# Ordering the second-layer loads behind the loads of h, and splitting up four tile turns, in an encoder layer on one core

## The chip, the core and the metric

The kernel runs on one core of a Trainium2 chip. The metric is the device time of one execution, in microseconds (us); the time before is the median of three runs, 2369.57 us (2364.59 to 2371.45).

## What is computed

One layer of a bidirectional encoder on 1024 tokens of width 1024, all in float32. Two of its four steps matter here, both feed-forward networks with a hidden width of 2816:

```python
def swiglu(x, w1, w3, w2):
    return (jax.nn.silu(x @ w1) * (x @ w3)) @ w2

x = layer_norm(ALPHA * x + 0.5 * swiglu(x, ffn1_w1, ffn1_w3, ffn1_w2), ln1_g, ln1_b)
...   # attention and a state-space branch, merged, then LN2
x = layer_norm(ALPHA * x + 0.5 * swiglu(x, ffn2_w1, ffn2_w3, ffn2_w2), ln3_g, ln3_b)
...   # a gated embedding, then LN4
```

## The kernel before, in words

**Products.** Every float32 matrix is held as a high and a low part (`split`, L62 to L65: the high part by ScalarE, the low part by VectorE), and a product is three TensorE matmuls: high by high, high by low, low by high. A matmul is 128x128 by 128x512. The large products use a seven-product scheme over 2x2 blocks, so each feed-forward matrix is cut in four blocks b11, b12, b21, b22, and sums and differences of blocks are made on VectorE.

**First pass, `ffn_up` (from L278).** For each of 11 column pairs p it forms the hidden values and, in its `finish` (L311), the seven left operands h, which are written to the DRAM tensor `hd` (L320, seven writes for each p). The last writes, of p = 10, are made while the second layer has begun.

**Second pass, `ffn_down` (L345 to L417).** It works through seven stages in the order 1, 5, 6, 3, 7, 2, 4 (`stages`, L377). A stage takes the 11 column pairs in six blocks q (`DUOS`: five of two, one of one). For each block it loads h (L393, `load_raw`, 512 KB, tag `raw`, four buffers), takes a block of w2, in four of the stages makes a difference of w2 blocks in place on VectorE first (L397), splits both, and then issues for each of four banks t the matmuls of L412. The four PSUM banks of a stage are added to `acc` at its end (L367 to L374, line L370). A block of two is 24 matmuls, a stage 132. The w2 blocks are loaded by `fetch` (L355, six loads at L361: four into the tile `w2w`, two into `w2e`): all six loads of b11 ahead of stage 1, of b12 ahead of stage 5, of b22 ahead of stage 6, of b21 ahead of stage 2. They go to tiles of the pools that the first pass frees at its end. The eight `acc` tiles (L549 from x, L975 from x2d) are loaded into the tiles that held the last hidden values; the norm's gain and bias (L110) into one more freed tile. h of block q = 5 in stage 1 can be loaded only when the writes of p = 10 have landed.

**The order of the work.** The program is traced into a scheduler, which fixes the order of each engine's instructions at compile time: an instruction that it takes to be ready goes in front of one that comes earlier in the program and isn't. Here all loads and stores are issued by SyncE (SP), one after the other, in that fixed order, and an instruction that waits holds up all behind it. A block `with tc.issue_after(ins)` keeps the order on one engine: what is traced in it stands behind `ins` in the engine's queue. It adds no wait on a result.

**The beginning of the second feed-forward (`first2`, L924 to L968).** Its input comes out of a layer norm, tile by tile of 128 tokens; `norm_in` (L183) runs the norm of tile j and turns tile j - 4 (`transpose_blocks`, L165: eight 128x128 transposes on TensorE into PSUM, then splits on ScalarE and VectorE into the tiles `xa` for j < 4, and `td` and `tc` for j from 4 on). So four turns, of tiles 4 to 7, are left for `finish` (L197). `first2` makes the first columns by plain products (`plain`, L260: two times 24 matmuls, with a `yield` after each 24): two of half 0, which read only `xa`; then `finish()`, L938, the four turns; then two of half 1, which read `td` and `tc`. Between parts of these it makes differences of `acc` (L176 to L181) and turns those (`turned`, L157).

Of the kernel before, what the change touches and what calls it, by code (L numbers as in the profile page):

```python
# [20 lines left out]
F32 = mybir.dt.float32  # L21
# [24 lines left out]
def layer_kernel(ctx, tc, A):  # L46
# [17 lines left out]
        S.activation(hi, src, AF.Copy)  # L64
        V.tensor_tensor(out=lo, in0=src, in1=hi.bitcast(F32), op=ALU.subtract)  # L65

    def load_raw(src, n=1024):
        raw = wts.tile([128, n], F32, tag="raw", bufs=RAW, name="raw")
        nc.sync.dma_start(raw, src)
        return raw  # L70

    def wload(src, tag="u", pool=None, bufs=None, n=1024):
# [34 lines left out]
    def ln_params(t, g, b):  # L107

        for i, src in enumerate((g, b)):
            nc.sync.dma_start(t[:, i, :], src.to_broadcast([128, D]))  # L110
        return t[:, 0, :], t[:, 1, :]
# [71 lines left out]
    def norm_in(steps, acc, gt, bt, xT, pool, done=None, lag=3, blocks=False):  # L183


        ready = []

        def bring(late):
            j = ready.pop(0)
            if blocks:  # L190
                transpose_blocks(acc, j, xT)
            else:
                transpose_in(acc[j], j, xT, late)
            if done:
                done(j)

        def finish():  # L197
            while ready:
                bring(True)

        for j, sums in steps:
            layer_norm(acc[j], sums, gt, bt, pool)
            ready.append(j)
            if len(ready) > lag:
                bring(False)
        return finish
# [53 lines left out]
    def plain(B, ws, half, row, s):  # L260


        u, g = [pdn.tile([128, 512], F32, tag="dn", name=n) for n in ("pu", "pg")]
        for i, b in enumerate(((B[1], B[2]), (B[4], B[3]))[half]):
            for k in range(4):
                ks = slice(i * 512 + k * 128, i * 512 + k * 128 + 128)
                for o, w in zip((u, g), ws):
                    wh, wl = w[row]
                    for m, (x, y) in enumerate(((wh, 0), (wh, 1), (wl, 0))):
                        PE.matmul(o, lhsT=x[:, ks], rhs=b[y][:, k, :], start=(i == 0 and k == 0 and m == 0),  # L270
                                  stop=(i == 1 and k == 3 and m == 2), skip_group_check=True)
            yield
        S.activation(s, u, AF.Silu)
        V.scalar_tensor_tensor(out=s, in0=s, scalar=0.5, in1=g, op0=ALU.mult, op1=ALU.mult)
# [67 lines left out]
                                   op0=ALU.mult, op1=ALU.mult)  # L342
            finish(p, s1, s2)

    def ffn_down(fp, acc, hd, w2, homes):  # L345

        W, ends = {}, {}
        sums = [sml.tile([128, 2], F32, tag="sums", bufs=8, name="sums") for _ in range(8)]

        def block(i, q):  # L350
            p, n = DUOS[q]
            t, o = (W[i], p) if p < 8 else (ends[i[0]], 3 * i[1] + p - 8)
            return t[:, o:o + n, :]

        def fetch(i):  # L355
            if i[0] not in ends:
                ends[i[0]] = homes["end", i[0]]("w2e", F32)
            W[i] = homes[i]("w2w", F32)
            for q in range(len(DUOS)):
                p, n = DUOS[q]  # L360
                nc.sync.dma_start(block(i, q), w2[i[0], i[1]][:, p:p + n, :])  # L361

        X = [pdn.tile([128, 512], F32, tag="dn", name="pd") for _ in range(4)]
        yt = []
        count = {}

        def add(out, j, n, ps, first, last):  # L367
            a = acc[j][:, n * 512:n * 512 + 512]
            if first or last:
                V.scalar_tensor_tensor(out=a, in0=a, scalar=ALPHA if first else 1.0, in1=ps, op0=ALU.mult, op1=ALU.add,  # L370
                                       accum_out=sums[j][:, n:n + 1] if last else None)
            else:
                V.tensor_tensor(out=a, in0=a, in1=ps, op=ALU.add)

        b11, b12, b21, b22 = (0, 0), (0, 1), (1, 0), (1, 1)

        stages = ((1, 0, True, [(0, 0, True, False)]), (5, 1, True, [(4, 1, True, False)]),  # L377
                  (6, 0, False, [(0, 1, True, False)]), (3, 1, False, [(0, 1, False, True)]),
                  (7, 0, False, [(4, 1, False, True)]), (2, 1, True, [(0, 0, False, True)]),
                  (4, 0, False, [(4, 0, True, True)]))  # L380
        want = {1: b11, 5: b12, 6: b22, 2: b21}
        right = {1: b11, 5: b11, 6: b11, 3: b22, 7: b12, 2: b21, 4: b11}
        less = {5: (b12, b11), 6: (b22, b11), 7: (b22, b12), 4: (b21, b11)}
        for i, bank, fresh, reads in stages:
            if i in want:
                fetch(want[i])
            if bank == 1 and fresh:
                yy = [pup.tile([128, 1024], F32, tag="up", name="pdy") for _ in range(2)]
                Y = [t[:, c:c + 512] for t in yy for c in (0, 512)]
            P = Y if bank else X  # L390
            held = []
            for q, (p, n) in enumerate(DUOS):
                h = load_raw(hd[i - 1][q].rearrange("p a b -> p (a b)")[:, 0:n * 512], n * 512)  # L393
                w = block(right[i], q)
                if i in less:
                    x, y = (block(b, q) for b in less[i])
                    V.tensor_tensor(out=w, in0=x, in1=y, op=ALU.subtract)  # L397
                hh, hl = [wts.tile([128, 1024], F32R, tag=t, name=o) for t, o in (("uh", "hh"), ("ul", "hl"))]
                wh, wl = [fp.tile([128, 1024], F32R, tag="v", bufs=4, name=o) for o in ("wh", "wl")]
                split(h[:, 0:n * 512], hh[:, 0:n * 512], hl[:, 0:n * 512])  # L400
                split(w, *[t[:, 0:n * 512].rearrange("p (a b) -> p a b", a=n) for t in (wh, wl)])
                held.append((p, n, hh, hl, wh, wl))
                if i == 4 and q == 4:
                    continue

                def part(t, first_p=held[0][0]):
                    for p, n, hh, hl, wh, wl in held:
                        for a in range(n):
                            ts = slice(a * 512 + t * 128, a * 512 + t * 128 + 128)
                            ws = slice(a * 512, a * 512 + 512)  # L410
                            for m, (x, y) in enumerate(((hh, wh), (hh, wl), (hl, wh))):
                                PE.matmul(P[t], lhsT=x[:, ts], rhs=y[:, ws], start=(fresh and p + a == 0 and m == 0),  # L412
                                          stop=(p + a == NP - 1 and m == 2), skip_group_check=True)

                for t in range(4):
                    part(t)
                    if q == len(DUOS) - 1:  # L417
                        for j, nn, first, last in reads:
                            add(None, j + t, nn, P[t], first, last)
                        if i == 4:  # L420
                            yield 4 + t, sums[4 + t]
                held = []
                if i == 4 and q < 4:
                    yield q, sums[q]

    def tok(t):
        return t.rearrange("(p j) d -> j p d", j=8)
# [37 lines left out]
    with tc.tile_pool(name="f1", bufs=1, reuse_waits="tile") as fp:  # L465
        def fx(name, dt=F32R, shape=(128, 8, 512)):
            return fp.tile(list(shape), dt, tag="x", bufs=3, name=name)
# [76 lines left out]

        acc = [fp.tile([128, 1024], F32, tag="a", bufs=8, name="acc") for _ in range(8)]
        homes = {(0, 0): fx, ("end", 0): fx, (0, 1): xx, (1, 1): xx, ("end", 1): xx, (1, 0): xx}
        dn = ffn_down(fp, acc, hd, A["ffn1_w2"], homes)
        for j in range(8):
            nc.sync.dma_start(acc[j], tok(A["x"])[j])  # L549

        def spill(j):
            nc.sync.dma_start(x1d[j], acc[j])

        first = next(dn)
        ln = ln_params(fx("ln", F32, (128, 2, 1024)), A["ln1_g"], A["ln1_b"])
        x1T = xtiles()
        finish = norm_in(chain([first], dn), acc, *ln, x1T, fp, spill)
        us = [("w_u", m, AF.Copy, ud) for m in range(4)]
# [365 lines left out]
    def first2():  # L924
# [7 lines left out]
                hl = wload(A[name][row * NP])  # L932
            w[i][row] = hl
        s1, s2 = [wts.tile([128, 1024], F32, tag="raw", bufs=RAW, name="raw") for _ in range(2)]
        for row, s in ((0, s1), (1, s2)):
            for _ in plain(X2b, w, 0, row, s[:, l]):
                pass
        finish()  # L938
        cs = [slice(c * 128, c * 128 + 128) for c in range(4)]
        c, last = 0, []  # L940
        for row, s in ((1, s2), (0, s1)):
# [16 lines left out]
        def ends():  # L958
# [3 lines left out]
            for c in (0, 2):  # L962
                t = turned((acc[c][:, r], acc[c + 1][:, r]))
                for i in range(2):
# [4 lines left out]
    ffn_up(fp, X2b, A["ffn2_w1"], A["ffn2_w3"], hd, first2)  # L969
    acc = [fa.tile([128, 1024], F32, tag="a", bufs=8, name="acc") for _ in range(8)]  # L970

    dn = ffn_down(fp, acc, hd, A["ffn2_w2"], {(0, 0): xx, ("end", 0): xx, (0, 1): xx, (1, 1): xx,
                                               ("end", 1): x16, (1, 0): x16})
    for j in range(8):
        nc.sync.dma_start(acc[j], x2d[j])  # L975
    first = next(dn)
    gt, bt = ln_params(x16("ln", F32, (128, 2, 1024)), A["ln3_g"], A["ln3_b"])
    x3T = [[f(n) for _ in range(2)] for f, n in ((xx, "xhi"), (x16, "xlo"))]
    finish = norm_in(chain([first], dn), acc, gt, bt, x3T, fp, lag=2)
    gt, bt = ln_params(x16("ln", F32, (128, 2, 1024)), A["ln4_g"], A["ln4_b"])  # L980
# [483 lines left out]
```

## Time and profile before

| | |
|---|---|
| median of three runs | 2369.57 us |
| the profiled execution: its time, its span | 2375.43 us, 2373.6 us |
| TensorE matmul busy | 2280.4 us, 96% of the span |
| VectorE busy | 1586.0 us, 67% |
| ScalarE busy | 938.4 us, 40% |
| moved by DMA | 265.63 MB, 112 GB/s over the span |
| mean granted TensorE clock | 0.982 |

The profile is of one execution. Its rows name engines as PE (TensorE matmul), DVE (VectorE), ACT (ScalarE), SPq (SyncE's queue, which issues the DMAs); L412 is line 412 of the kernel; `out<-in` are the program's names of the tiles. The granted clock is a share of 2.4 GHz. Times within the execution are counted from the start of the span. The first feed-forward's second pass lies at about 435 to 660 us, the second one's at about 2000 to 2225 us; `first2` begins at about 1555 us.

### The profile page before, as it was taken

The page shows a single profiled execution, that of the slowest core. Times are in us where ns is not written, and L with a number is a line of the kernel's source. Part 1 is how long each engine was busy: PE and PEld are TensorE (multiplying, and loading weights), DVE is VectorE, ACT ScalarE, POOL GpSimd, SP SyncE. Part 2 cuts the span into 40 slices and gives each one's busy share as a digit, 9 for nine tenths or more (in the row PEclk, how much of TensorE's full clock was granted, in tenths as well). Part 3 has the DMA queues.
Part 4 walks back from the last instruction along what each step waited for, and adds up shares of the span by engine and source line. Part 5 has one row for each costly group of instructions (what it writes and reads, how often), then busy time and mean ns, then how long its engine had stood idle before and what let it go on. Part 6 is the DMA issues. An engine that isn't in the chain of part 4 may idle for free.

```text
span 2373.6 us, 28494 instructions
## 1 busy us (share of the span) xinstructions
PE 2280.4 (96%) x10784; PEld 1876.8 (79%) x10784; DVE 1586.0 (67%) x2388; ACT 938.4 (40%) x1344; POOL 390.2 (16%) x419
## 2 busy tenths in 40 slices
PE   8999999999989989998999999989999999999897
PEld 7888888777768778886888888778888888777686
DVE  7565646665667899948688876665655646664836
ACT  5333333333432322234477871234333333233525
POOL 0000000000009455515255542000000000000000
PEclk9999999999999989998999999989999999999999
DMA  4332323932234222344100025122323327622211
GB/s 158 109 106 94 123 77 124 358 120 91 97 133 151 95 65 91 114 157 182 52 10 26 29 113 190 36 80 76 124 86 107 115 92 266 235 94 98 90 40 72
DMA packets 103899, 265.63 MB, mean 112 GB/s; under 512 B 13264, under 2 KB 27856, under 8 KB 103760
## 3 DMA queue, kind: packets, MB, share of 16 engines
q1 hardware_dynamic: 103760, 263.80, 32.3%
q8 instruction: 85, 1.39, 0.2%
q14 instruction: 54, 0.44, 0.1%
HBM read 189.33 MB, written 74.42 MB: 111 GB/s over the span
## 4 chain that ended last, share of the span: by engine, by line
PE 83%; DVE 7%; DMA 4%; issue 2%; ACT 2%; POOL 1%; SPq 0%; DVEq 0%; ACTq 0%; POOLq 0%
PE px L232 18%; PE pg L84 11%; PE py L232 9%; PE pdy L412 8%; PE pd L412 7%; PE pz L232 5%; PE pd L84 3%; PE pgate L84 3%; PE ps L84 3%; PE pov L706 2%; PE pu L270 2%; PE pg L270 2%; PE tpp L693 2%; PE pya L84 2%; DMA w2w<-in_ffn_w_dram 2%
## 5 line engine op out<-in xcount | busy, mean ns | idle before, releaser
L65 DVE TENSOR_TENSOR wlo<-raw,whi 128x1024 fp32r<-128x1024 f32 (+4 forms) x116 | 145.0, 1255 | 68.8 <-ACT whi L64 66.1
L64 ACT ACTIVATE whi<-raw 128x1024 fp32r<-128x1024 f32 (+4 forms) x116 | 112.3, 974 | 187.0 <-PE pg L84 111.4
L84 PE MATMUL pg<-xhi,whi 128*128 128x512 f32 x416 | 164.1, 395 | 0.1
L84 PE MATMUL pg<-xlo,whi 128*128 128x512 f32 x416 | 163.6, 393 | 0.3 <-DVE t L1201 0.3
L84 PE MATMUL pg<-xhi,wlo 128*128 128x512 f32 x416 | 162.9, 392 | 0.0
L412 PE MATMUL pd<-wl,hh 128*128 128x512 f32 x352 | 142.9, 406 | 6.0 <-DVE wl L65 6.0
L412 PE MATMUL pd<-wh,hl 128*128 128x512 f32 x352 | 140.9, 404 | 0.0
L412 PE MATMUL pd<-wh,hh 128*128 128x512 f32 x352 | 123.6, 404 | 7.5 <-ACT hh L64 6.6
L64 ACT ACTIVATE wh<-w2w 128x1024 fp32r<-128x1024 f32 x56 | 59.3, 1058 | 168.2 <-PE pd L412 84.2
L1232 POOL MEMSET T1r<- 128x32 f32 x1 | 0.2, 160 | 652.9 <-DMA x1d<-acc 652.9
L232 PE MATMUL py<-tch,fhl 128*128 128x512 f32 x320 | 106.0, 392 | 0.0
L412 PE MATMUL pdy<-wl,hh 128*128 128x512 f32 x264 | 104.4, 395 | 0.0
L412 PE MATMUL pdy<-wh,hl 128*128 128x512 f32 x264 | 103.9, 395 | 0.0
L65 DVE TENSOR_TENSOR hl<-raw,hh 128x1024 fp32r<-128x1024 f32 x84 | 94.9, 1132 | 11.3 <-ACT hh L64 11.2
L412 PE MATMUL pdy<-wh,hh 128*128 128x512 f32 x264 | 100.0, 396 | 0.0
L232 PE MATMUL px<-td,thi 128*128 128x512 f32 x320 | 98.8, 390 | 0.0
L64 ACT ACTIVATE fhl<-raw 128x512 fp32r<-128x512 f32 x40 | 25.3, 633 | 179.9 <-PE px L232 177.3
L65 DVE TENSOR_TENSOR wl<-w2w,wh 128x1024 fp32r<-128x1024 f32 x56 | 68.4, 1221 | 39.1 <-ACT wh L64 38.9
L680 POOL TENSOR_SCALAR P<-P,sm 128x1024 f32<-128x1024 f32 x64 | 74.8, 1170 | 117.1 <-DVE sm L679 98.4
L65 DVE TENSOR_TENSOR pt<-tpp,pt 128x512 fp32r<-128x512 f32 x128 | 85.6, 684 | 11.7 <-ACT pt L64 10.3
L84 PEld LDWEIGHTS pg<-xhi,whi 128*128 128x128 f32 x416 | 78.5, 189 | 17.2 <-issue 1.0
L84 PEld LDWEIGHTS pg<-xlo,whi 128*128 128x128 f32 x416 | 78.6, 189 | 16.8 <-DVE xlo L65 0.8
(431 smaller groups left out, 6395.0 us busy)
## 6 DMA issues: line engine op xcount, KB each, us to landing
raw<-in_ffn_w_dram SPq DMA_DIRECT2D x86, 512.0 KB, 3.7
raw<-hd SPq DMA_DIRECT2D x70, 512.0 KB, 3.3
hd<-c SPq DMA_DIRECT2D x88, 256.0 KB, 3.6
w2w<-in_ffn_w_dram SPq DMA_DIRECT2D x32, 512.0 KB, 8.6
hd<-s SPq DMA_DIRECT2D x60, 256.0 KB, 3.3
rawx<-in_xT_dram SPq DMA_DIRECT2D x16, 256.0 KB, 6.4
w2e<-in_ffn_w_dram SPq DMA_DIRECT2D x8, 512.0 KB, 8.8
acc<-in_x_dram SPq DMA_DIRECT2D x8, 512.0 KB, 8.8
```

The source lines that it names most:

```text
L64: S.activation(hi, src, AF.Copy)
L65: V.tensor_tensor(out=lo, in0=src, in1=hi.bitcast(F32), op=ALU.subtract)
L84: PE.matmul(out, lhsT=a, rhs=b, start=(n == 0), stop=(n == last))
L232: PE.matmul(out, lhsT=x[:, ks], rhs=y[:, k, :], start=(first and n == 0), stop=(n == 11), skip_group_check=True)
L270: PE.matmul(o, lhsT=x[:, ks], rhs=b[y][:, k, :], start=(i == 0 and k == 0 and m == 0), stop=(i == 1 and k == 3 and m == 2), skip_group_che ...
L412: PE.matmul(P[t], lhsT=x[:, ts], rhs=y[:, ws], start=(fresh and p + a == 0 and m == 0), stop=(p + a == NP - 1 and m == 2), skip_group_chec ...
L680: G.tensor_scalar(out=P, in0=P, scalar1=sm, scalar2=1.0, op0=ALU.mult, op1=ALU.mult)
L693: PE.transpose(tp[:, k * 128:k * 128 + 128], P[:, (q * 4 + k) * 128:(q * 4 + k) * 128 + 128], idt)
L706: PE.matmul(p[:, 0:256], lhsT=vt[:, k, c0:c0 + 128], rhs=pt[k // 4][b][:, k % 4, :], start=(k == 0 and b == 0), stop=(k == 7 and b == 1))
L1232: G.memset(T[0][:, :, 0], 1.0)
```

## The change

Three things, the first two in both second passes.

**h is loaded one step ahead.** A new list `hs` collects the h loads. The first h load of each stage but the first is traced in the last block of the stage ahead of it (`ahead`, `follows`).

**Other loads are tied behind h loads.** The fetch of b11 stays at the front. The fetches of b12, b22 and b21 are traced at block q = 2 of the stage ahead of the one that they were fetched for, each load behind the h load issued last (`behind`). The loads of `acc` 0 to 3 are traced at q = 4 of stage 1, those of `acc` 4 to 7 at q = 4 of stage 5, in the same way. The norm's two parameter loads stand behind the h load that is eighth from the end when the first tile is done.

**Turns between plain products.** In `first2` the turns of tiles 4 and 5 are made after the first plain product of half 0, those of tiles 6 and 7 after the first 24 matmuls of the second one.

```diff
-    def load_raw(src, n=1024):
+    def load_raw(src, n=1024, note=None):
         raw = wts.tile([128, n], F32, tag="raw", bufs=RAW, name="raw")
-        nc.sync.dma_start(raw, src)
+        dma = nc.sync.dma_start(raw, src)
+        if note is not None:
+            note.append(dma)
         return raw
...
-        def finish():
-            while ready:
+        def finish(n=8):
+            while ready and n:
                 bring(True)
+                n -= 1
...
-    def ffn_down(fp, acc, hd, w2, homes):
+    def ffn_down(fp, acc, x0, hd, w2, homes, hs):
...
-                nc.sync.dma_start(block(i, q), w2[i[0], i[1]][:, p:p + n, :])
+                behind(lambda: nc.sync.dma_start(block(i, q), w2[i[0], i[1]][:, p:p + n, :]))
+
+        def behind(load):
+            if hs:
+                with tc.issue_after(hs[-1].ins):
+                    load()
+            else:
+                load()
...
+        follows = {1: 5, 5: 6, 6: 3, 3: 7, 7: 2, 2: 4}
+        ahead = None
+
+        def hload(i, q):
+            n = DUOS[q][1] * 512
+            return load_raw(hd[i - 1][q].rearrange("p a b -> p (a b)")[:, 0:n], n, hs)
...
-            if i in want:
+            if i == 1:
                 fetch(want[i])
...
-                h = load_raw(hd[i - 1][q].rearrange("p a b -> p (a b)")[:, 0:n * 512], n * 512)
+                if q == 0:
+                    h = ahead or hload(i, 0)
+                else:
+                    h = hload(i, q)
+                if q == len(DUOS) - 1 and i != 4:
+                    ahead = hload(follows[i], 0)
+                if q == 2 and i != 4 and follows[i] in want:
+                    fetch(want[follows[i]])
+                if q == 4 and i in (1, 5):
+                    for j in range(4):
+                        behind(lambda: nc.sync.dma_start(acc[j + (i == 5) * 4], x0[j + (i == 5) * 4]))
...
         first = next(dn)
-        ln = ln_params(fx("ln", F32, (128, 2, 1024)), A["ln1_g"], A["ln1_b"])
+        with tc.issue_after(hs[-8].ins):
+            ln = ln_params(fx("ln", F32, (128, 2, 1024)), A["ln1_g"], A["ln1_b"])
...
-        for row, s in ((0, s1), (1, s2)):
-            for _ in plain(X2b, w, 0, row, s[:, l]):
-                pass
-        finish()
+        for _ in plain(X2b, w, 0, 0, s1[:, l]):
+            pass
+        finish(2)
+        for _ in plain(X2b, w, 0, 1, s2[:, l]):
+            finish(2)
```

The two loops that loaded `acc` ahead of the first step of `ffn_down` (L549, L975) are gone, and the second feed-forward's parameters of LN3 are tied like those of LN1.

## Rows read from the trace of the kernel before

**Rows 1.** The page, part 4: shares of the chain that ended last

```profile
PE 83%; DVE 7%; DMA 4%; issue 2%; ACT 2%; POOL 1%; SPq 0%; DVEq 0%; ACTq 0%; POOLq 0%
```

**Rows 2.** Waits of PE, whole span: waiter, releaser, us in total, times, longest

```profile
PE pd L412 <- ACT hh L64: 6.6, 2, 3.8
...
PE pd L412 <- DVE wl L65: 6.0, 6, 2.0
...
PE tln L162 <- DVE tcl L65: 4.1, 2, 3.6
```

**Rows 3.** Chain of waits, 400 to 660 us: start, us, what

```profile
464.08 6.95 DMA raw<-hd
...
471.73 5.49 PE pd L412 x12
477.21 29.73 PE pdy L412 x126
...
515.86 24.44 PE pd L412 x104
```

**Rows 4.** Stretches ahead of and around the stall: us, busy of each engine, PEclk, DMA share, GB/s

```profile
430.00:464.00 34.00, 34.00 (x148) 27.67 (x147) 27.85 (x29) 10.28 (x12) 0.00 (x0) 1.00 1.03 414
464.00:478.00 14.00, 11.15 (x36) 8.54 (x36) 9.38 (x12) 5.81 (x6) 0.00 (x0) 0.76 1.03 418
```

**Rows 5.** The same stall in the second feed-forward: timeline of PE, then the chain

```profile
2036.70 0.50 PE L412 MATMUL pd<-wh,hh 128*128 128x512 f32 x1 [3.79 <-ACT hh L64]
...
2036.70 4.61 PE pd L412 x12
```

**Rows 6.** Timeline of SP's queue, 395 to 640 us: start, us, what it issues

```profile
432.47 4.87 SPq L361 DMA_DIRECT2D w2w<-in_ffn_w_dram  x8
...
449.02 0.33 SPq L320 DMA_DIRECT2D hd<-s  x1
...
462.24 0.33 SPq L320 DMA_DIRECT2D hd<-c  x1
...
464.08 2.85 SPq L69 DMA_DIRECT2D raw<-hd  x4
...
472.88 162.70 SPq L69 DMA_DIRECT2D raw<-hd  x33
```

**Rows 7.** The page, part 6: issues, KB each, median us to landing

```profile
raw<-hd SPq DMA_DIRECT2D x70, 512.0 KB, 3.3
...
w2w<-in_ffn_w_dram SPq DMA_DIRECT2D x32, 512.0 KB, 8.6
```

**Rows 8.** Timeline of DVE, 430 to 485 us

```profile
441.86 1.22 DVE L397 TENSOR_TENSOR w2w<-w2w 128x1024 f32<-128x1024 f32 x1
...
448.81 0.69 DVE L317 TENSOR_TENSOR c<-s,c 128x512 f32<-128x512 f32 x1
...
475.97 2.48 DVE L370 SCALAR_TENSOR_TENSOR acc<-acc,pd 128x512 f32<-128x512 f32 x4
```

**Rows 9.** Timeline of PE around the four turns; brackets: idle before it, and what ended it

```profile
1578.55 1.91 PE L162 MATMUL tln<-idt,acc 128*128 128x128 f32 x16
1584.09 1.94 PE L162 MATMUL tln<-idt,acc 128*128 128x128 f32 x8 [3.63 <-DVE tcl L65]
...
1589.18 0.80 PE L270 MATMUL pu<-td,whi 128*128 128x512 f32 x1 [0.74 <-ACT td L64]
...
1591.81 0.79 PE L270 MATMUL pu<-td,whi 128*128 128x512 f32 x1 [0.56 <-DVE td L65]
...
1599.55 1.04 PE L162 MATMUL tln<-idt,acc 128*128 128x128 f32 x8
```

**Rows 10.** Timeline of DVE in the same stretch

```profile
1563.01 2.47 DVE L133 SCALAR_TENSOR_TENSOR acc<-acc,ln,ln 128x1024 f32<-128x1024 f32 x2
...
1578.82 0.69 DVE L274 SCALAR_TENSOR_TENSOR raw<-raw,pg 128x512 f32<-128x512 f32 x1 [10.21 <-PE pg L270]
...
1585.66 0.68 DVE L65 TENSOR_TENSOR tcl<-tln,tch 128x512 fp32r<-128x512 f32 x1
```

More of the change, by code (lines that the diff above doesn't have):

```diff
@@ L360, in fetch @@
                 p, n = DUOS[q]
-                nc.sync.dma_start(block(i, q), w2[i[0], i[1]][:, p:p + n, :])
-        X = [pdn.tile([128, 512], F32, tag="dn", name="pd") for _ in range(4)]
-        yt = []
-        count = {}
+                behind(lambda: nc.sync.dma_start(block(i, q), w2[i[0], i[1]][:, p:p + n, :]))
[5 more added lines that the diff above has]
+                load()
+        X = [pdn.tile([128, 512], F32, tag="dn", name="pd") for _ in range(4)]
+        follows = {1: 5, 5: 6, 6: 3, 3: 7, 7: 2, 2: 4}
[3 more added lines that the diff above has]
+            return load_raw(hd[i - 1][q].rearrange("p a b -> p (a b)")[:, 0:n], n, hs)
         def add(out, j, n, ps, first, last):
@@ L546, in layer_kernel @@
         homes = {(0, 0): fx, ("end", 0): fx, (0, 1): xx, (1, 1): xx, ("end", 1): xx, (1, 0): xx}
-        dn = ffn_down(fp, acc, hd, A["ffn1_w2"], homes)
-        for j in range(8):
-            nc.sync.dma_start(acc[j], tok(A["x"])[j])
+        hs = []
+        dn = ffn_down(fp, acc, tok(A["x"]), hd, A["ffn1_w2"], homes, hs)
         def spill(j):
@@ L970, in layer_kernel @@
     acc = [fa.tile([128, 1024], F32, tag="a", bufs=8, name="acc") for _ in range(8)]
[L972 to L975, printed above, removed]
+    hs = []
+    dn = ffn_down(fp, acc, x2d, hd, A["ffn2_w2"], {(0, 0): xx, ("end", 0): xx, (0, 1): xx, (1, 1): xx,
+                                               ("end", 1): x16, (1, 0): x16}, hs)
     first = next(dn)
-    gt, bt = ln_params(x16("ln", F32, (128, 2, 1024)), A["ln3_g"], A["ln3_b"])
+    with tc.issue_after(hs[-8].ins):
+        gt, bt = ln_params(x16("ln", F32, (128, 2, 1024)), A["ln3_g"], A["ln3_b"])
     x3T = [[f(n) for _ in range(2)] for f, n in ((xx, "xhi"), (x16, "xlo"))]
```

## The prediction

> **What bounds the kernel now.** I read the chain that ended last first: 83% of the span is TensorE, 4% DMA [rows 1]. So the kernel is as long as TensorE's work plus what TensorE loses to gaps and to a low clock, and a change is worth what it takes out of these. Next the waits of TensorE, for gaps that lie where the change does: the second pass has two waits for `hh`, the high part of h, 6.6 us together and 3.8 us the longest, and the turns have two waits for `tcl`, 4.1 us [rows 2]. Most other long waits of TensorE lie in places that the change doesn't touch.
>
> The chain through the first second pass says what makes `hh` late: ScalarE waits for an h load issued at 464.08 us that takes 6.95 us [rows 3], where such a load takes 3.3 us by the median [rows 7]. The stretches say why: from 430 to 464 us the DMA engines are full (share 1.03, 414 GB/s), and in the next 14 us TensorE gets 36 matmuls done at a granted clock of 0.76, a mean over its two levels, 1.2 and 2.4 GHz [rows 4]. SP's queue shows what fills them: behind eight `w2w` loads from 432.47 us on come all other w2 blocks, `acc` and the norm's parameters; the h loads come last, at 464.08, behind the last write of h at 462.24. From 472.88 on the queue has 33 h loads in 162.7 us and nothing else [rows 6]. So the w2 blocks of the whole pass and `acc`, some 14 MB (34 us at 414 GB/s), go out ahead of a load that is needed at once. The second feed-forward has the same stall, 3.79 us [rows 5].
>
> **The change, part by part.** Sums are made against the profiled execution, 2375.43 us, which is 0.25% over the median; I take the difference off the median, 2369.57.
>
> *The stall of the first feed-forward.* After the gap of 2.85 us (the 6.6 of [rows 2] less the 3.79 of [rows 5], to rounding) 12 matmuls take 5.49 us; at full clock 104 take 24.44, so 0.235 each and 2.82 for 12 [rows 3]. Loss: 2.85 + 2.67 = **5.5 us**.
>
> *The stall of the second.* The gap is 3.79 us, and 12 matmuls then take 4.61 instead of 2.82 [rows 5]: 3.79 + 1.79 = **5.6 us**.
>
> Does the change take them away? b11 and b12 are still loaded at once, about 5.8 MB, since b12 stands behind an h load (stage 1, q = 2) that is out early. b22, b21, four `acc` tiles and the parameters, some 9 MB or 22 us at 414 GB/s, move behind h loads that wait for a `raw` buffer. What bounds the late h load then is the last write of h. VectorE has its operand ready at 448.81 + 0.69 = 449.5 [rows 8]; the write could go then instead of at 462.24, and landing (about 3 us each for the write and the load) brings h at some 456 us, 12 us before the gap at 468.9 begins. So I take the whole loss as gained. The bounds: all of it, or nothing, if the queue's fixed order keeps the load where it is.
>
> *What is loaded later.* A fetch is six loads, 2.9 MB, 7 us with full DMA engines [rows 4], 8.6 us for one load in the worst crowd [rows 7]. With four `raw` buffers an h load goes out when the block four ahead is split, so b22 leaves while stage 1 is being multiplied, one stage (132 matmuls, 31 us by [rows 3]) ahead of stage 6; b21 leaves two stages ahead of stage 4 and some 25 us ahead of stage 2. `acc` 0 to 3 are first read at 475.97 [rows 8] and wait, as before, for tiles that the writes of h free by about 460; `acc` 4 to 7 have a stage more. The parameters are read only after stage 4 has begun. In SP's queue each tied load stands behind an h load that waits for a buffer; behind it wait later h loads alone, and SP's issue costs 0.33 us of a queue with 4.9 us to each load [rows 6]. VectorE's differences come later too: the first stands at 441.86 [rows 8], among work for the last h. Cost: nothing, hidden under 20 us and more of products; without that cover it would be a stall like the one removed, 5.6 us for each fetch.
>
> *h one step ahead.* The order of h loads and the four buffers stay. Nothing.
>
> *The turns.* The 16 transposes of two tiles start at 1578.55, the next two turns wait 3.63 and 0.47 us (4.1 in [rows 2]) for PSUM tiles to be split, and the products of half 1 wait 0.74 and 0.56 for the last splits: 5.40 us of gaps [rows 2, 9]. Behind the long gap everything is slow: eight transposes take 1.94 us where, at 1599.55, eight take 1.04 and 16 take 1.91, so about 0.9 for eight; the two slow turns cost 2.1 us more. From 1589.18 to 1599.55 there are 26 matmuls in 10.37 us; less the 0.56 gap and 26 x 0.235 = 6.1, that is 3.7 more. Loss: 5.4 + 2.1 + 3.7 = **11.2 us**.
>
> After the change the same 32 transposes stand between plain products that need only `xa`. The norms of all tiles are written by 1563.01 + 2.47 = 1565.5, before the first plain product ends, and VectorE then idles 10.21 us up to 1578.82 [rows 10], so the splits of tiles 4 and 5 have room. Behind the last turn 24 matmuls remain, 5.6 us, for the splits of tiles 6 and 7. Before, the splits of two tiles ended at 1585.66 + 0.68, 5.9 us after their turns, mixed with differences of `acc` [rows 9, 10]. So the cover falls short by 0.3 us at most. ScalarE, POOL and SP get nothing new.
>
> *The sum.* 5.5 + 5.6 + 11.2 = 22.3 us. I take off 0.3 for the splits and 1.0, one wait of the kind that the second pass has at stage changes (6.0 us in six [rows 2]), for what is late next: VectorE's `wl`. That leaves **21.0 us**: 2354.4 against the profiled execution, **2348.6** against the median. TensorE is full behind each of the three places, so what is gained there reaches the end.
>
> **The rivals.** *A. As forecast*, 2344 to 2354: 0.70.
>
> *B. The h load stays late.* The queue's order is fixed ahead of time, and the tie only says what stands behind an h load, not that the load of block q = 5 moves forward; `acc` 0 to 3 are tied ahead of it and wait for the tiles that the h writes free. For it: before, the h loads stand behind every write of h. Against: those writes were themselves held up by full DMA engines. The change then does only half of what it says: 11.2 - 0.3 = 10.9 gained, 2358.7. Chance 0.12.
>
> *C. The turns still stall.* VectorE mixes the splits with differences and TensorE waits at the same place: 11.1 - 1.0 = 10.1 gained, 2359.5. The idle 10.21 us speak against it. Chance 0.06.
>
> *D. The tied loads come late.* VectorE runs in a fixed order; a difference placed on the belief that a w2 block is there holds up every split behind it, and TensorE stands. The place is the first difference of stages 5, 6 and 7, and it decides once a fetch lands later than VectorE arrives, over 20 us after the tied load by the working above. Price: 5.6 us for each fetch, three in each pass. One or two late: 2355 to 2360, chance 0.05. All six late: 33.6 - 21.0 = 12.6 slower, 2382; chance 0.03. Against it: the loads of h, issued four blocks ahead, hold with 3.3 us to landing. The Trainium skill speaks for D: the page "DMA: Bandwidth & Descriptors", section "Rules for kernel authors", says to issue a DMA early and wait for it late so that its setup is covered, and this change issues 18 loads a pass later than it could. By that rule the kernel would lose as in D; the full DMA engines of [rows 4] show that early has a price here too.
>
> *E. Nothing is left of it*, through a new order in the tails of the second passes (the fixed order may change anywhere behind an edit): 2369, chance 0.04.
>
> **How the numbers follow.** Predicted is A's 2348.6. The low end adds some 5 us for tails that happen to come out better, 2343; the high end holds B, 2360. D's bad end and E, 0.07, lie outside, with some of the rest. About 0.3%, or 7 us, is what a measurement of this kernel can tell from no change. Faster by more: A, B, C and the mild D, 0.93, less a little for errors in the terms: 0.91. Within: 0.05. Slower: 0.04.
>
> **What would show it.** Right: in SP's queue the first two fetches only before the last h writes, the h loads of stage 1 out by about 455 us, no wait of `pd` for `hh`, and in 464 to 478 us a granted clock of 1.00 with over 55 matmuls. No wait for `tcl` at the turns, and TensorE's clock at 1.00 up to the first `td` product. Wrong: the wait for `hh` still there (B); waits of `wl` or `w2w` on DMA in stages 5 to 7 (D); a gap ahead of the first `td` product (C).

## The result, and the profile after

The changed kernel takes **2347.82 us** (median of four runs, 2345.81 to 2348.71) against 2367.93 of the kernel before beside it: a ratio of 0.9914, with a 95% interval from 0.9897 to 0.9931. Timed a second time it came to 2345.45 against 2369.32, a ratio of 0.9904 (0.9891 to 0.9918). 20 us are gained in the first comparison; 21.0 were forecast, to 2348.6.

The chain that ended last answers to [rows 1]: DMA has gone from 4% of the span to 1%.

```profile
PE 87%; DVE 7%; ACT 2%; issue 2%; DMA 1%; POOL 1%; SPq 0%; DVEq 0%; ACTq 0%
```

Of the waits of PE over the whole span [rows 2], that of `pd` for `hh` and that of `tln` for `tcl` are not in the list any more. The wait of `pd` for `wl` is what it was, and a small one is new, of `pdy` for `wl`:

```profile
PE pd L439 <- DVE wl L65: 6.0, 6, 2.0
...
PE pdy L439 <- DVE wl L65: 0.8, 2, 0.4
```

The stretches of [rows 4] (us, busy time of PE, PEld, DVE, ACT and POOL, granted clock, DMA share, GB/s):

```profile
430.00:464.00 34.00, 34.00 (x148) 27.64 (x147) 24.58 (x27) 11.72 (x14) 0.00 (x0) 1.00 0.98 373
464.00:478.00 14.00, 13.60 (x59) 10.71 (x58) 14.00 (x16) 4.99 (x6) 0.00 (x0) 1.00 0.73 268
```

Where TensorE did 36 matmuls it now does 59, at full clock. The DMA engines are still nearly full ahead of it, 373 GB/s. What has changed is the order, as SP's queue shows [rows 6]:

```profile
431.80 1.75 SPq L367 DMA_DIRECT2D w2w<-in_ffn_w_dram  x4
...
441.68 1.69 SPq L420 DMA_DIRECT2D acc<-in_x_dram  x3
...
445.63 1.35 SPq L69 DMA_DIRECT2D raw<-hd  x2
448.19 1.68 SPq L323 DMA_DIRECT2D hd<-c  x2
450.30 4.77 SPq L69 DMA_DIRECT2D raw<-hd  x2
455.17 1.81 SPq L367 DMA_DIRECT2D w2w<-in_ffn_w_dram  x4
...
549.21 1.93 SPq L367 DMA_DIRECT2D w2w<-in_ffn_w_dram  x4
```

The late h load (the last of stage 1, 256 KB) goes out at 445.6 us instead of 464.1, still ahead of the last writes of h. It takes 7.7 us to land, no less than before, and is there at 453.3; its split on ScalarE stands at 457.81 and not at 471.04. b22 follows at 455, b21 at 549.

From the first turn on, TensorE's timeline has no bracket left, that is, no wait [rows 9]; the first line stands ahead of the turns:

```profile
1549.60 0.80 PE L273 MATMUL pu<-xal,whi 128*128 128x512 f32 x1 [0.76 <-DVE ln L129]
...
1561.68 1.91 PE L164 MATMUL tln<-idt,acc 128*128 128x128 f32 x16
...
1571.78 1.91 PE L164 MATMUL tln<-idt,acc 128*128 128x128 f32 x16
...
1581.88 1.03 PE L164 MATMUL tln<-idt,acc 128*128 128x128 f32 x8
```

To see where the time went, both spans are cut at TensorE's landmarks: the first or last start of a group of matmuls. The columns are the lengths between the first `pd<-wh,hh` (stage 1), the first `pdy<-wh,hh` (stage 5), the first `pg<-xhi,whi` (the projections), the last `pg<-xhi,wlo`, the last `pd<-whi,ml` (the end of the middle part), the last `pg<-tch,wlo` (the end of `first2`), the last `px<-td,tlo` (the end of the second first pass), the last `pdy<-wh,hl` (stage 2) and the last `pd<-wh,hl` (stage 4), and from there to the end of the span; in us, one profiled execution each. The experiments that the lower rows belong to come in the next section.

| kernel | stage 1 | rest of pass | projections | middle | first2 | ffn_up | 2nd pass to stage 2 | stage 4 | end |
|---|---|---|---|---|---|---|---|---|---|
| before | 41.7 | 207.4 | 368.6 | 499.0 | 66.2 | 387.1 | 197.3 | 33.3 | 137.7 |
| after | 36.2 | 206.5 | 368.6 | 498.7 | 56.2 | 387.1 | 192.6 | 31.7 | 134.7 |
| after, second profile | 36.2 | 207.6 | 368.7 | 498.4 | 56.3 | 387.1 | 192.5 | 31.6 | 134.7 |
| turns alone | 39.2 | 206.8 | 368.6 | 492.4 | 54.7 | 387.2 | 197.1 | 33.2 | 136.9 |
| ties alone | 36.2 | 206.5 | 368.6 | 492.7 | 65.9 | 387.1 | 192.4 | 31.8 | 134.6 |
| acc in front | 36.2 | 206.1 | 368.8 | 498.8 | 56.2 | 387.1 | 192.1 | 31.7 | 134.8 |
| acc in front, second profile | 36.1 | 206.1 | 368.4 | 492.6 | 54.7 | 387.1 | 192.1 | 33.2 | 134.4 |
| w2 untied | 38.6 | 205.5 | 368.7 | 498.0 | 56.3 | 387.1 | 193.9 | 33.3 | 136.9 |
| b21 alone tied | 37.9 | 207.4 | 368.8 | 495.5 | 54.7 | 387.1 | 191.5 | 33.2 | 136.1 |
| w2 late | 36.1 | 214.6 | 369.1 | 493.1 | 54.6 | 387.2 | 198.9 | 31.7 | 134.9 |
| b22 later | 36.2 | 207.6 | 368.9 | 494.7 | 54.7 | 387.1 | 194.8 | 33.3 | 137.0 |
| second pair at the end | 36.2 | 207.8 | 368.8 | 492.5 | 56.4 | 387.1 | 192.4 | 33.3 | 136.8 |

Of the change itself: 5.5 us in stage 1, 4.7 in the second pass, 10.0 in `first2`. The two profiled spans differ by 26.7 us, more than the medians. Of the rest 0.7 lies ahead of stage 1, 0.9 in the rest of the first pass, and 4.6 in stage 4 and the end. The last is not one lucky execution: the second profile of the changed kernel has it too. The transposes of the last norm stand in another order there. Before, 16 go in one run at a low clock (3.65 us, where 16 take 1.91 at full clock [rows 9]); in the changed kernel they go eight at a time, at full clock. First the kernel before, stretch and TensorE's timeline, then the changed one:

```profile
2236.60:2257.60 21.00, 15.24 (x59) 11.35 (x58) 19.74 (x40) 11.42 (x16) 0.00 (x0) 0.84 0.45 159
2248.88 3.65 PE L146 MATMUL tln<-idt,acc 128*128 128x128 f32 x16 [1.11 <-DVE ln L127]
```

```profile
2214.50:2235.50 21.00, 15.09 (x68) 11.35 (x69) 18.12 (x38) 10.46 (x14) 0.00 (x0) 1.00 0.53 171
2226.51 1.06 PE L148 MATMUL tln<-idt,acc 128*128 128x128 f32 x8 [1.61 <-DVE ln L129]
```

The edit doesn't touch this place. The turns alone, w2 untied, b22 later and the second pair at the end have the order of the kernel before, and all have 33.2 or 33.3 us in stage 4 and 136.8 to 137.0 behind it. The ties alone have the order of the changed kernel and its times. So some 4 us come and go with the order that the scheduler happens to choose, though no run changes that order alone. In stage 4 it isn't the order alone: `acc` in front has 31.7 and 33.2 there in two profiles of one kernel. The middle part, which nobody touched either, takes 492 to 499 us; of that below.

### The profile page after: what moved, and what is told of

The parts are those of the page before. It is cut to its first block, busy times and chain, and to the rows that moved or that the text cites. A ratio compares the mean times of both kernels' runs of the same rounds, so it can differ in the third digit from the quotient of the medians.

```text
span 2346.9 us, 28488 instructions
## 1 busy us (share of the span) xinstructions
PE 2266.6 (97%) x10784; PEld 1866.7 (80%) x10784; DVE 1582.8 (67%) x2388; ACT 936.6 (40%) x1344; POOL 389.4 (17%) x419
## 4 chain that ended last, share of the span: by engine, by line
PE 87%; DVE 7%; ACT 2%; issue 2%; DMA 1%; POOL 1%; SPq 0%; DVEq 0%; ACTq 0%
PE px L235 19%; PE pg L86 11%; PE py L235 9%; PE pd L439 8%; PE pdy L439 8%; PE pz L235 5%; PE pd L86 3%; PE pgate L86 3%; PE ps L86 3%; PE pov L733 2%; PE pu L273 2%; PE pg L273 2%; PE tpp L720 2%; PE pya L86 2%; PE pyb L86 2%
## 5 line engine op out<-in xcount | busy, mean ns | idle before, releaser
L86 PEld LDWEIGHTS pg<-xhi,wlo 128*128 128x128 f32 x416 | 78.4, 189 | 16.1
```

Source lines behind the costliest of these rows:

```text
L86: PE.matmul(out, lhsT=a, rhs=b, start=(n == 0), stop=(n == last))
```

## The experiments

**The two parts alone.** The first kernel is the one before with the new turns; the second is the changed one with `finish()` back behind both plain products.

```diff
 # turns alone, on the kernel before
-        for row, s in ((0, s1), (1, s2)):
-            for _ in plain(X2b, w, 0, row, s[:, l]):
-                pass
-        finish()
+        for _ in plain(X2b, w, 0, 0, s1[:, l]):
+            pass
+        finish(2)
+        for _ in plain(X2b, w, 0, 1, s2[:, l]):
+            finish(2)
```

> The kernel before with the turns alone changed. Theory (the three places are independent, and TensorE is full behind each): the profile of the changed kernel gains 10.0 us between the start of first2 and its end, so about 2358 us against 2367.9 before; the waits of pd for hh stay at 2.9 and 3.8 us, the wait for tcl is gone. Rival (part of the gain at the turns comes from what the earlier loads left on VectorE and in the queue): under 6 us gained, above 2362.

> The changed kernel with the four turns as before. Theory: the two waits for hh are gone, 4.8 us each by the landmarks of the changed kernel, so 9.6 gained, about 2358; the wait for tcl of 4.1 us is back with the slow stretch behind it. Rival (the ties give back in the tails what they gain): under 5 us gained, above 2363.

The turns alone: 2358.17 against 2369.95, 0.9952 (0.9934 to 0.9969), so 11.8 us. The ties alone: 2356.17, 0.9942 (0.9920 to 0.9964), 13.8 us. Together that is 25.6, of which the interval of each leaves 4 or 5 open, against 20 to 24 for the whole change: no sign that the parts need or hinder each other. (Both came out as expected; in the 13.8 of the ties are the 4 us at the end of the kernel.) In the waits of PE of the turns alone, 430 to 640 us, the old stall stands:

```profile
PE pd L413 <- ACT hh L64: 2.7, 1, 2.7
```

But the clock stays up behind it, unlike before (0.50 us for the first matmul where the kernel before has 0.80, TensorE's timelines):

```profile
471.73 0.80 PE L412 MATMUL pd<-wh,hh 128*128 128x512 f32 x1 [2.85 <-ACT hh L64]
...
471.27 0.50 PE L413 MATMUL pd<-wh,hh 128*128 128x512 f32 x1 [2.73 <-ACT hh L64]
```

In the waits of the ties alone, 1530 to 1625 us, the old wait at the turns stands:

```profile
PE tln L164 <- DVE tcl L65: 4.1, 2, 3.6
```

The stretches agree: `first2` takes 54.7 us with the new turns and 65.9 without, stage 1 36.2 with the ties and 39.2 without. The 39.2 are 2.5 us less than before, with the same gap: that is the low clock behind it, which this execution hadn't.

**Which of the ties is it?** In one kernel only the w2 blocks are tied, in one only `acc` and the parameters, in one b21 alone. Turns and early h loads are as in the changed kernel.

```diff
 # acc and parameters in front
-                if q == 4 and i in (1, 5):
-                    for j in range(4):
-                        behind(lambda: nc.sync.dma_start(acc[j + (i == 5) * 4], x0[j + (i == 5) * 4]))
...
+        for j in range(8):
+            nc.sync.dma_start(acc[j], tok(A["x"])[j])
 # w2 in front
-            if i == 1:
+            if i in want:
                 fetch(want[i])
-                if q == 2 and i != 4 and follows[i] in want:
-                    fetch(want[follows[i]])
 # b21 alone: acc and parameters in front, and
-            if i == 1:
+            if i in (1, 5, 6):
                 fetch(want[i])
...
-                if q == 2 and i != 4 and follows[i] in want:
+                if q == 2 and i == 7:
                     fetch(want[follows[i]])
```

> The changed kernel with the loads of acc and of the norm's parameters traced where they were before; only the w2 blocks stay behind h loads. Theory (what counts is how many loads stand ahead of the late h load, at about 1.1 us each with full DMA engines): the 12 loads of b22 and b21 are out of the way, 13 us, more than the gap of 2.9 to 3.8 us, so no wait for hh, 2347 to 2350. Rival (acc is what holds the queue, since it waits for tiles that the writes of h free): the wait for hh is back at 2 to 4 us in both passes, 2356 to 2358.

> The changed kernel with all fetches of w2 where they were before, untied; acc and the parameters stay behind h loads. Theory (the count of loads ahead): about seven loads of acc and parameters fewer ahead of the late h load, 8 us, still more than the gap, so no wait for hh here either, 2347 to 2351: either half of the ties would do. Rival (the w2 blocks alone make the crowd): the wait is back at 2 us or more, 2354 to 2358.

> Only the fetch of b21 tied; b12, b22, acc and the parameters stand where they stood before; turns as changed. Theory (the count of loads ahead of the late h load, about 1.1 us each): six loads fewer bring it 6 to 7 us forward, to 457 or 458 us, more than the gap, so the wait for hh is gone or under 0.5 us, 2346 to 2351. Rival (all loads that aren't needed soon must go): half of the gap stays, 1.5 us or more with a low clock behind it, 2352 to 2357.

> The changed kernel itself, timed again beside the next three. Theory and rivals alike: 2346 to 2349, with the two waits for hh gone.

> The kernel with only the w2 fetches tied, acc and the parameters in front, again. Theory (acc and the parameters need no tie; the 4 us by which it was faster are executions that happened to keep the clock up): within 2 us of the changed kernel timed beside it, 2345 to 2349. Rival (acc in front is better, since the queue is busy with it while it waits for h anyway): 3 us or more faster than the changed kernel, 2344 or less.

With `acc` and the parameters in front: 2343.65 (0.9884, 0.9864 to 0.9903), and in the second timing 2347.99 (0.9908, 0.9894 to 0.9922) beside 2345.45 of the changed kernel. There is no wait for `hh` in either, so the rival that `acc` holds the queue falls. So does the other, that `acc` in front is better: the 4 us of the first timing were no gain.

With w2 in front: 2349.44 (0.9916, 0.9896 to 0.9936), by its time not to be told from the changed kernel. The profile does tell: half of the gap is left, in both passes, which I had not expected. My count was wrong first of all. Since `acc` 0 to 3 are tied to an h load that is out early, they still stand ahead; only three loads had gone, and the h loads go out at 461.05 and not at 464.08, 1.0 us for each load. With b21 alone tied: 2347.62 (0.9906, 0.9890 to 0.9921); six loads fewer ahead, and the h loads at 457.52, 1.1 us for each. The count of loads is right, the time is what I expected, and yet in the first pass 1.43 us of gap stay in both kernels. TensorE's timeline with w2 in front:

```profile
469.92 0.50 PE L437 MATMUL pd<-wh,hh 128*128 128x512 f32 x1 [1.43 <-ACT hh L64]
...
472.52 0.72 PE L437 MATMUL pd<-wh,hl 128*128 128x512 f32 x2 [0.47 <-DVE hl L65]
```

and with b21 alone:

```profile
469.87 0.50 PE L439 MATMUL pd<-wh,hh 128*128 128x512 f32 x1 [1.43 <-ACT hh L64]
```

In that kernel the h load lands at 457.5 + 7.2 = 464.7, more than 3 us before TensorE runs dry at 468.4. The timeline of ACT says what it waits for, in the first pass and then in the second:

```profile
462.67 0.63 ACT L64 ACTIVATE wh<-w2e 128x512 fp32r<-128x512 f32 x1 [4.52 <-PE pd L439]
468.24 1.06 ACT L64 ACTIVATE wh<-w2w 128x1024 fp32r<-128x1024 f32 x1 [4.94 <-PE pd L439]
469.20 1.56 ACT L64 ACTIVATE hh<-raw 128x512 fp32r<-128x512 f32 x2
...
2008.11 0.63 ACT L64 ACTIVATE wh<-w2e 128x512 fp32r<-128x512 f32 x1 [4.52 <-PE pd L439]
2008.64 1.56 ACT L64 ACTIVATE hh<-raw 128x512 fp32r<-128x512 f32 x2
2013.68 1.06 ACT L64 ACTIVATE wh<-w2w 128x1024 fp32r<-128x1024 f32 x1 [3.47 <-PE pd L439]
```

In the first pass the split of the late h (`hh`, 128x512) stands behind the split of the next stage's w2 block, and that waits 4.94 us for TensorE to give up a buffer. So the split waits for TensorE, and TensorE then waits for the split. In the second pass of the same kernel the two stand the other way round, and there is no gap. The kernel before had the bad order too:

```profile
468.67 1.06 ACT L64 ACTIVATE wh<-w2w 128x1024 fp32r<-128x1024 f32 x1 [4.94 <-PE pd L412]
471.04 0.63 ACT L64 ACTIVATE hh<-raw 128x512 fp32r<-128x512 f32 x1 [1.31 <-DMA raw<-hd]
```

Here the data landed at 471.03 only, so a better order alone would have given nothing; an earlier load alone is worth 1.42 of the 2.85 us, and the other 1.43 take the order too. The changed kernel has the good one:

```profile
457.81 0.61 ACT L64 ACTIVATE hh<-raw 128x512 fp32r<-128x512 f32 x1
462.43 0.63 ACT L64 ACTIVATE wh<-w2e 128x512 fp32r<-128x512 f32 x1 [4.00 <-PE pd L439]
...
468.00 1.06 ACT L64 ACTIVATE wh<-w2w 128x1024 fp32r<-128x1024 f32 x1 [3.99 <-PE pd L439]
```

That the scheduler chose the order by when it believed the h load to be there fits the passes shown here, but its belief isn't in a trace, so this stays argued.

**h one step ahead.** The changed kernel without the early trace of the next stage's first h load:

```diff
-                if q == len(DUOS) - 1 and i != 4:
-                    ahead = hload(follows[i], 0)
```

> The changed kernel without the load of h one step ahead; the ties stay. Theory: the order of h loads and the four buffers decide, not where the load is traced, so no change, 2346 to 2350. Rival (it is the early trace of the next stage's first h that keeps it in front of the tied loads): a wait for hh at the starts of stages 5, 6 and 2, 0.5 to 3 us each, 2351 to 2360.

2346.45 (0.9900, 0.9881 to 0.9920), the same stretches, no new wait. This part does nothing for the time by itself.

**Later loads.** In one kernel the fetches are traced at the start of their own stage, behind its fourth h load; in the other only b22's moves, from block 2 to block 4 of stage 5.

```diff
 # w2 late
+            early = {}
             if i == 1:
                 fetch(want[i])
+            elif i in want:
+                early = {q: hload(i, q) for q in (1, 2, 3)}
+                fetch(want[i])
 # b22 later
-                if q == 2 and i != 4 and follows[i] in want:
+                if q == (4 if i == 5 else 2) and i != 4 and follows[i] in want:
```

> The changed kernel with the fetches of b12, b22 and b21 later: traced at the start of their own stage, behind that stage's fourth h load. Theory (cover of a stage and more was ample, cover of two blocks is just used up): the fetch goes out about 12 us ahead of its stage, lands in 6 to 9, and the difference and the split take 3.5 more, so each of six costs 0 to 2 us on VectorE, 2348 to 2360. Rival (a late fetch costs what the old stall cost): 5 us or more for each, 2378 or more.

> The changed kernel with the fetch of b22 traced at block q = 4 of stage 5 instead of q = 2. Theory (the 0.4 us wait for wl at the start of stage 5 comes from differences with b22 that VectorE makes ahead of the split, the first of them waiting for its load): with b22 later, those differences move behind the split, the 0.4 us wait goes in both passes, 2346 to 2348. Rival (the wait has to do with the additions to acc, not with b22): the wait of 0.4 us stays, or b22 is now late and stage 6 waits, 2348 to 2352.

Late: 2357.14 (0.9951, 0.9930 to 0.9973), 9 to 12 us slower than the two timings of the changed kernel, and inside the range that I gave. By the table it is 7 to 8 us in the rest of the first pass (214.6; the two profiles of the changed kernel have 206.5 and 207.6) and 6.3 in the second. But the six fetches don't share it evenly, and my 0 to 2 us for each is wrong. At the change to stage 6 VectorE makes six differences with b22 in one go; the addition to `acc` and the split that TensorE needs stand behind them. VectorE's timeline, then TensorE's:

```profile
497.23 6.89 DVE L426 TENSOR_TENSOR w2w<-w2w 128x1024 f32<-128x1024 f32 x6
...
504.77 0.50 PE L441 MATMUL pdy<-wh,hh 128*128 128x512 f32 x1 [2.17 <-DVE acc L387]
507.04 0.80 PE L441 MATMUL pd<-wl,hh 128*128 128x512 f32 x1 [1.30 <-DVE wl L65]
```

A low clock follows. In the 13 us from 503 us on TensorE does 28 matmuls, and in the same piece of the changed kernel 52; 24 matmuls are 5.6 us at full clock. First w2 late, then the changed kernel:

```profile
503.00:516.00 13.00, 9.72 (x28) 7.18 (x29) 11.65 (x14) 1.67 (x2) 0.00 (x0) 0.74 0.08 27
```

```profile
502.00:515.00 13.00, 12.29 (x52) 9.36 (x51) 7.66 (x9) 4.34 (x5) 0.00 (x0) 1.00 0.25 84
```

The second pass has the same two gaps, 2.20 and 1.31 us, at the same place. The late b21 costs a wait of 1.92 us in the first pass and 0.51 in the second, the late b12 0.1 in each. So the rival's price, 5 us or more, is right for b22 and wrong for the others.

b22 later: 2350.99 (0.9931, 0.9916 to 0.9945), about 5 us behind the changed kernel beside it, as the rival had it by its time. The 0.40 us wait at the start of stage 5 is gone, as the theory had it, but two others stand in its place in both passes: the differences with b22 now stand ahead of the next splits. The late load of b22 accounts for 2.3 of the 5 us at most, in the second pass (194.8 against 192.5 in the changed kernel's second profile). Another 4.0 lie in stage 4 and the end (33.3 and 137.0 against 31.6 and 134.7), where this kernel has the order of transposes of the kernel before; other stretches of this execution came out shorter. VectorE also waits 2.2 us for a w2 load, at 2102 us, but that is b21, and TensorE waits 0.5 us behind it. TensorE's timeline:

```profile
478.42 0.50 PE L439 MATMUL pdy<-wl,hh 128*128 128x512 f32 x1 [1.25 <-DVE wl L65]
...
484.70 0.50 PE L439 MATMUL pdy<-wl,hh 128*128 128x512 f32 x1 [0.44 <-DVE wl L65]
```

**Where the turns stand.** All four behind the first product in one kernel; in the other the second pair at the very end.

```diff
 # in one block
-        finish(2)
+        finish(4)
         for _ in plain(X2b, w, 0, 1, s2[:, l]):
-            finish(2)
+            pass
 # second pair at the end
         for _ in plain(X2b, w, 0, 1, s2[:, l]):
-            finish(2)
+            pass
+        finish(2)
```

> The changed kernel with all four turns traced after the first plain product, and the second one whole behind them. Theory (the gap at the turns came from nothing being left to multiply while the PSUM tiles are split): the scheduler fills the wait between the second and the third turn with matmuls of the second product, so no loss, 2346 to 2350. Rival (the place in the program decides, turns in one block wait for PSUM): the wait for tcl of 3 to 4 us and a low clock behind it, 2352 to 2358.

> The changed kernel with the turns of tiles 6 and 7 at the end, after the second plain product, those of 4 and 5 between the two. Theory (the last 24 matmuls cover the last splits): without them the first product on td waits about 2 to 3 us for splits, with or without a low clock behind it: 2350 to 2354. Rival (only the wait for PSUM between the second and third turn mattered): 2346 to 2349.

In one block: 2346.97 (0.9902, 0.9885 to 0.9919), no loss. TensorE's timeline shows why: the scheduler put 8 us of products between the second and the third turn by itself, and from 1555 to 1578 us TensorE has no gap.

```profile
1558.33 1.91 PE L164 MATMUL tln<-idt,acc 128*128 128x128 f32 x16
...
1568.43 1.91 PE L164 MATMUL tln<-idt,acc 128*128 128x128 f32 x16
```

```profile
1555.00:1578.00 23.00, 23.00 (x118) 19.26 (x117) 18.90 (x30) 5.66 (x10) 0.00 (x0) 1.00 0.31 116
```

With the second pair at the end: 2350.08 (0.9916, 0.9901 to 0.9931). The first products on `td` wait, as expected, but 1.15 us and not 2 to 3, and the clock stays up behind it (0.50 us for the first matmul, where [rows 9] has 0.80). `first2` takes 56.4 us, 1.7 more than with the turns spread; the rest of its time over the changed kernel fits stage 4 and the end, where it too has the order of before (33.3 and 136.8). So the wait for PSUM tiles between the second and third turn, with the low clock behind it, made up nearly all of the 11 us, and the cover at the end under 2.

```profile
1570.85 0.50 PE L273 MATMUL pu<-td,whi 128*128 128x512 f32 x1 [0.69 <-ACT td L64]
...
1572.51 0.50 PE L273 MATMUL pu<-td,whi 128*128 128x512 f32 x1 [0.46 <-DVE td L65]
```

None of the experiments beats the changed kernel by more than the measurement leaves open.

## Why the prediction was right

**The three places.** The forecast took them as independent and TensorE as full behind each; both held. The two parts alone give 11.8 and 13.8 us, and the stretch behind the turns (387.1 or 387.2 us for the second `ffn_up` in every kernel) didn't move.

**The stall of the first feed-forward**, 5.5 us forecast: stage 1 is 5.5 us shorter. Of the forecast 2.67 were the low clock behind the gap, and that isn't there in every execution: against the turns alone, with the gap and without the low clock, the ties gain 3.0 us in stage 1 (39.2 to 36.2). The cause was half seen. That the h load stands behind loads that aren't needed yet is shown, at 1.0 to 1.1 us for each load ahead of it. Two things were not right. What was said to bound the late load then, the last write of h, doesn't: the load of stage 1 reads what one of the seven writes of p = 10 puts down, not all of them, and it goes out at 445.63 us, ahead of the last two writes at 448.19, so it was there at 453.3 and not at 456. And ScalarE's fixed order was not looked at: without that order coming right the earlier load would have given back only part. With b21 alone tied, stage 1 takes 37.9 us and not 36.2. That the order came right in the changed kernel was not foreseen.

**The stall of the second**, 5.6 forecast: 4.7 to 4.9 came (197.3 to between 192.4 and 192.6). 0.4 of the rest is the new wait below; the last few tenths were not traced.

**What is loaded later**, forecast at nothing: about 0.4 us in each pass, the new wait of `pdy` for `wl`, together less than the 1.0 taken off for what is late next. VectorE makes differences with b22 ahead of that split, as its timeline in the changed kernel shows:

```profile
466.58 2.35 DVE L424 TENSOR_TENSOR w2w<-w2w 128x1024 f32<-128x1024 f32 x2
468.85 1.21 DVE L424 TENSOR_TENSOR w2e<-w2e 128x1024 f32<-128x1024 f32 x1
...
470.59 1.21 DVE L65 TENSOR_TENSOR wl<-w2w,wh 128x1024 fp32r<-128x1024 f32 x1
```

It doesn't wait for the load there: its two waits for w2 in this pass, 0.8 us each, come at 555.8 and 557.8, for b21, and TensorE has no gap behind them. That is rival D at a small scale, with one difference: what holds up the split is not the wait for a block but the work on it. The margin is smaller than the stage and more of my working: issued 11 us later (466.18 instead of 455.17), b22 already added 1.3 us of waits to the first pass, and 37 us later (492.23) it cost what D said, about 5.6 us with a low clock behind the gaps. For the other late fetches that price was too high, 0.1 to 1.9 us. The Trainium skill spoke for D: the page "DMA: Bandwidth & Descriptors", section "Rules for kernel authors", says to issue a DMA early. The runs bear that out for the fetches that were moved too far (9 to 12 us lost), and not for those of the kernel before, where early loads stood in front of an urgent one.

**The turns**, 11.2 less 0.3 forecast: `first2` is 10.0 us shorter in the profile of the changed kernel, and 11.5 in six other profiles with the new turns (54.6 to 54.7), where the clock stayed up at its beginning. In both profiles of the changed kernel and in three of other kernels it did not (56.2 to 56.3); the sign that TensorE's clock is at 1.00 up to the first `td` product failed there, at a place ahead of the turns. The 0.3 for splits that end late did not appear.

**B** fell by the queue's row, 445.63, and the worry that `acc` 0 to 3 would hold the load with it: they do stand ahead, but from 441.68 us on. **C** fell by the brackets that are missing. **E** named the tails of the second passes as a risk; they moved the other way, 1.6 us in stage 4 and 3.0 behind it, and by less than 1 in the rest of the first pass.

**How much of the agreement is luck.** The three places give 20.2 us in the profiles, with the mechanisms forecast. That the first median comes within a microsecond of 2348.6 is more than the working could promise: the 4.6 us at the end were in no term, part of the losses to the low clock varies with the execution, and the second timing gained 23.9 us and not 20.1.

## What to carry to other kernels

Where one queue issues all loads, look at what stands ahead of the load that TensorE waits for, and count it; each load ahead of it, most of them 512 KB, cost it a microsecond here, and moving three or six of those that are needed later already brought the data in time. Then look at the engines between that load and TensorE: here an instruction placed behind one that itself waits for TensorE brought half of the stall back though the data was there. Before a load is moved back, look at the work that another engine does on it: b22, from which VectorE makes the differences of two stages, was the dear one. Work that waits for PSUM tiles to be emptied wants independent products around it; here the scheduler filled them in by itself when they came later in the program. And compare the places that the edit does not touch: a new fixed order there was worth 4 us.

## What the runs showed of the hardware that I had not expected

The same gaps are or are not followed by a low clock, from one execution to the next. At the beginning of `first2` TensorE waits 1.15 or 1.16 us and then 0.76 to 0.78 us in all kernels. Behind that the changed kernel ran at a granted clock of 0.79, a mean over the two levels of 1.2 and 2.4 GHz, and the kernel with the turns alone at 1.00; first the changed one:

```profile
1547.80:1556.00 8.20, 7.38 (x24) 5.62 (x25) 8.20 (x26) 4.78 (x9) 0.00 (x0) 0.79 0.20 83
```

```profile
1545.30:1553.50 8.20, 7.39 (x31) 5.83 (x32) 8.20 (x26) 4.78 (x8) 0.00 (x0) 1.00 0.20 83
```

24 matmuls against 31 in 8.2 us, which is the difference between 56.2 and 54.7 us of `first2`. That it is the execution and not the program is shown by the kernel with `acc` in front, which was profiled twice: 56.2 and 54.7 us. The middle part varies at a larger scale, in code that no kernel here changes: the stretch from the last `pg` product to the last `pglu` takes 36.9 us in one of these two profiles of the same kernel and 33.6 in the other, at a granted clock of 0.86 and 0.90.

```profile
1046.10:1083.00 36.90, 27.33 (x105) 21.13 (x104) 25.37 (x20) 14.23 (x21) 14.55 (x6) 0.86 0.58 217
```

```profile
1045.50:1079.10 33.60, 25.83 (x103) 20.26 (x102) 22.65 (x17) 13.51 (x21) 15.18 (x6) 0.90 0.64 239
```

TensorE is busy 1.5 us longer for about as many matmuls. Of the rest 1.64 us is a wait of `pk` for `mx` that only the longer one has; what makes it come and go was not looked into.

This makes 6 us of spread in the middle and 1.5 to 2.5 us in several other places, about what the runs of one kernel differ by. Two profiled spans alone would have put the gain at 26.7 us instead of 20 to 24.
